# A four-layer mixer kernel: S5's direct term in its convolution kernels, z in three matmuls per block of rows, last state matrices loaded early, S5's parameter steps one head later

## The chip, the cores and the metric

One core of a Trainium2 chip runs the whole program in one launch. The metric is the device time of that launch in microseconds (us), as a median over runs. Engines: PE is TensorE (PEld its weight loads), DVE VectorE, ACT ScalarE, POOL GpSimd, SP SyncE (here only a DMA queue).

## The reference, cut to what matters

Input x is 1 x 256 x 2048, fp32. Four layers follow each other (SSD, FOX, MLA, S5), each a mixer between a residual and a LayerNorm. The change touches SSD's scores, the heads of FOX and above all S5:

```python
def s5_mixer(h, w_in, lam_re, lam_im, log_step, b_re, b_im, c_re, c_im, d_skip, w_glu, b_glu, w_out):
    u, z = jnp.split(h @ w_in, 2, axis=-1)
    ...                                   # lam_bar, b_bar from the parameters, u in groups of 16
    bu = jnp.einsum('gpi,btgi->btgp', b_bar, ug)
    _, states = lax.associative_scan(_diag_linear_combine, (a_seq, bu), axis=1)
    y = jnp.einsum('gip,btgp->btgi', c, states).real.reshape(bsz, T, S5_WIDTH) + d_skip.astype(f32) * u
    y = jax.nn.gelu(y)
    y = y * jax.nn.sigmoid(y @ w_glu.astype(f32) + b_glu.astype(f32))
    y = y * jax.nn.silu(z.astype(f32))
    return y.astype(h.dtype) @ w_out
```

## The kernel before, in words

**Products.** Every fp32 product with a weight is made of three products of halves: high x high, high x low, low x high. A half tile of weights (512 KB, `raw`, 7 buffers) is loaded by SP's queue; ACT rounds it to `whi` (L119) and DVE subtracts to get `wlo` (L120), 4 buffers each. Activations lie transposed, 16 blocks of 128 rows x 256 tokens, as a high and a low part, side by side as well.

`proj_T` (L153) makes 128 output features x 256 tokens: for each of the 16 blocks one 512-wide matmul of `whi` against [high | low] (L147) and one 256-wide matmul of `wlo` against high (L148). The result has two halves of 256 columns, which a DVE reduction adds (L157). `proj_Tk` (L200) has another form, three 256-wide matmuls per block into one sum (L212 to L214), with nothing left to add. `proj_tok` (L160) makes token-major outputs by `mm3` (L126 to L128).

**Order.** The engines' instruction streams are in the order that a scheduler gives them. The kernel's own clock is `C.tick()`: it passes once for each half tile of weights in the projections named here. `C.defer(n, fn)` runs `fn` n ticks later and puts its instructions behind the last matmul issued so far, so that small work of a layer is dealt out among the matmuls.

**SSD.** In each of eight groups `scores` (L557) multiplies the decay matrices `arena` (made at L538) by C·B (L567, DVE); it is deferred by three ticks (L569).

**FOX.** While FOX runs, the parameters of S5 are prepared by a generator, `s5_params`, in 16 turns. One step of it is POOL work for turn n (L1101 to L1126, ending in the matrices `pn`, whose state part is written to `P_d` in DRAM, L1132) and PE work for turn n - 1 (`turn`, L1053: four transposes L1057 and 16 small matmuls L1064 that give the convolution kernels `kt`, copied from PSUM by DVE at L1066). Eight steps are deferred, three come behind v strips, and each head takes one more (L715). POOL also makes the head's mask `ckm` (L714), behind `C.pool_last`, the last step's DMA.

**S5.** Four u strips come first (`proj_Tk`), then 16 tiles of z (`z_tile`, by `proj_T`), each followed by a tanh on ACT and one DVE operation (L1324). Under the matmuls of z run: the state recurrence on DVE (`scan`, L1194 to L1200, four kinds of operations), dealt out by `advance` at SCAN_US = 1.9 of its own estimate per tick; and `outputs`, which takes k = 0 to 7 (four feature tiles ft, two halves each) as soon as the states of the tile are done: `y_near` (kernels against u, L1383), `y_far` (state matrices against states, L1399, added by DVE at L1403), `back1` and `back2` (transposes L1412, L1422). In `back2` DVE adds the direct term D·u (L1428), and one tick later `gelu` follows. Kernels and state matrices for k come by POOL's DMA queue into three buffers of one tag, "mats" (`shifts` L1175, `mats` L1166). After z, PE goes on with the gate's projection (glu), whose tiles take the feature tile ft = 3 last, then with the output layer.

Of the kernel before, what the change touches and what calls it, by code (L numbers as in the profile page):

```python
# [30 lines left out]
class Core:  # L31
# [104 lines left out]
    def proj_T_steps(self, src, hT, ps, m=P, order=range(KB)):  # L136

        mm = self.nc.tensor.matmul
        for i in range(2):
            w = self.half(src, i, KB * m)
            for j in range(8):
                kb = 8 * i + j
                hi, lo = (x[:, j * m:(j + 1) * m] for x in w)
                mm(ps, hi, hT[2][order[kb]], start=kb == 0, stop=False)  # L147
# [303 lines left out]
def ssd(C, hT, out):  # L451
# [3 lines left out]
    with C.tc.tile_pool(name="ssd", bufs=1) as sp, C.tc.tile_pool(name="ssd_c", bufs=1) as vp, C.tc.tile_pool(name="ssd_t", bufs=1) as tp:  # L455
# [87 lines left out]
        def group(g):  # L543
# [25 lines left out]
            C.defer(3, scores)  # L569
# [85 lines left out]
def fox(C, hT, out):  # L655
# [3 lines left out]
    with pool(name="fox", bufs=1) as fp, pool(name="fox_t", bufs=2) as tp, \  # L659
# [49 lines left out]
        def head(h):  # L709
# [5 lines left out]
            C.behind(lambda: next(steps, None))  # L715
# [218 lines left out]
def s5_params(C, sp, sq):  # L934
# [118 lines left out]
    def turn(n, st, pn, d):  # L1053
# [12 lines left out]
        V.tensor_copy(kt[n % 2][:, :, 48:], kp[0:64, 0:128].rearrange("p (e f) -> p e f", e=2))  # L1066
# [74 lines left out]
def s5(C, hT, out):  # L1141
# [8 lines left out]
    with C.tc.tile_pool(name="s5", bufs=1) as sp, C.tc.tile_pool(name="s5_w", bufs=1) as wp, C.tc.tile_pool(name="s5_t", bufs=1) as tp:  # L1150
        dT = sp.tile([P, KB], F32, name="dT")
        bg = sp.tile([P, KB], F32, name="bg")
        nc.sync.dma_start(dT, A["s5_dT"])
# [175 lines left out]
        held = []  # L1329

        def y_load(k):
            ft, h2 = divmod(k, 2)
# [4 lines left out]

        def outputs():
# [92 lines left out]
        def gelu(ft, yf):  # L1431
            y4 = sp.tile([P, 2, 4, T], F32R, tag=f"xu{ft}", name=f"y4{ft}")
            for gq in range(4):
                kb = 4 * gq + ft
                yh[kb], yl[kb], yb[kb] = y4[:, 0, gq], y4[:, 1, gq], y4[:, :, gq]
                g = tp.tile([P, T], F32, tag="gl", name="gl", bufs=2)
                nc.scalar.activation(g.rearrange("p (m k r) -> p r k m", k=4, r=L), yf[gq].rearrange("p (r k m) -> p r k m", r=L, k=4),
                                     AF.Gelu_apprx_tanh)
                C.split(yh[kb], yl[kb], g)
# [53 lines left out]
def prep(inp):  # L1493
# [75 lines left out]
```

## Time and profile before

| | us |
|---|---|
| three runs | 2040.04, 2040.04, 2044.45 (median 2040.04) |
| profiled execution, its own time | 2042.04 |
| its span in the trace | 2040.2 |
| PE busy | 1988.5 (97% of the span) |
| DVE busy | 1472.4 (72%) |
| ACT busy | 957.6 (47%) |
| POOL busy | 409.7 (20%) |

How to read it: the profiled execution lasted 2 us more than the median, so a change of the profiled time is taken over to the median as a difference. Busy times overlap; on PE the ends of matmuls are modelled, so spacings from start to start are safer than durations. The granted clock (PEclk) is 1.00 at 2.4 GHz and 0.50 at 1.2 GHz.

### The profile page before, as it was taken

What the parts mean: (1) busy time and instruction counts of PE and PEld (TensorE: products, weight loads), DVE (VectorE), ACT (ScalarE), POOL (GpSimd) and SP (SyncE); (2) the same over time, 40 slices, a digit from 0 to 9 for tenths busy, and PEclk for the clock granted to TensorE, in tenths of its full rate; (3) what the DMA queues carried; (4) which work ended last, traced back from release to release, by engine and by line L of the source; (5) the groups of instructions that cost most, each with busy time, mean ns of one, the idle gap of its engine ahead of it and who ended that gap; (6) DMA issues with size and microseconds to landing.
All of it is one profiled execution on the core that took longest, in us unless ns stands there. A gap on an engine that the chain in (4) does not pass through costs nothing.

```text
span 2040.2 us, 31823 instructions
## 1 busy us (share of the span) xinstructions
PE 1988.5 (97%) x12073; PEld 1695.5 (83%) x12073; DVE 1472.4 (72%) x2572; ACT 957.6 (47%) x1427; POOL 409.7 (20%) x482
## 2 busy tenths in 40 slices
PE   8999999999999999999999999999999999999997
PEld 6788888888888878788888879888888799778885
DVE  6798887887644695677776567766556678996856
ACT  5455555555433334344444444545554355445542
POOL 0101111001100018999991000000000000110002
PEclk9999999999999999999999999999999999999999
DMA  8555555555665547565666555654347556685652
GB/s 285 186 184 181 185 176 184 186 185 185 218 200 191 181 139 242 182 205 198 197 209 197 180 183 150 205 190 145 104 145 252 174 184 197 171 250 194 196 191 91
DMA packets 116233, 382.40 MB, mean 187 GB/s; under 512 B 18208, under 2 KB 20976, under 8 KB 114288
## 3 DMA queue, kind: packets, MB, share of 16 engines
q1 hardware_dynamic: 103424, 348.11, 52.5%
q0 software_dynamic: 7808, 26.56, 4.2%
q10 hardware_dynamic: 4848, 5.70, 0.8%
q8 instruction: 95, 1.56, 0.3%
q14 instruction: 58, 0.48, 0.1%
HBM read 366.20 MB, written 14.11 MB: 186 GB/s over the span
## 4 chain that ended last, share of the span: by engine, by line
PE 82%; DVE 10%; DMA 3%; POOL 2%; issue 2%; ACT 1%; SPq 0%; DVEq 0%; POOLq 0%; ACTq 0%
PE pT L147 24%; PE pT L148 12%; PE pt L127 10%; PE pt L126 10%; PE pt L128 10%; DVE wlo L120 3%; PE pk L212 2%; PE pk L214 2%; PE pk L213 2%; PE yd L602 1%; PE lps L898 1%; PE lps L897 1%; DVE hres L339 1%; DVE hres L340 1%; PE o L444 1%
## 5 line engine op out<-in xcount | busy, mean ns | idle before, releaser
L120 DVE TENSOR_TENSOR wlo<-raw,whi 128x1024 fp32r<-128x1024 f32 (+4 forms) x612 | 751.5, 1230 | 340.4 <-ACT whi L119 336.4
L119 ACT CAST whi<-raw 128x1024 fp32r<-128x1024 f32 (+4 forms) x612 | 632.0, 1036 | 730.9 <-PE pt L128 316.9
L147 PE MATMUL pT<-h,whi 128*128 128x512 f32 (+2 forms) x2080 | 744.8, 401 | 0.0
L148 PE MATMUL pT<-h,wlo 128*128 128x256 f32 (+2 forms) x2080 | 585.4, 281 | 3.0 <-DVE wlo L120 3.0
L147 PEld LDWEIGHTS pT<-h,whi 128*128 128x128 f32 (+2 forms) x2080 | 389.6, 187 | 92.8 <-issue 0.2
L148 PEld LDWEIGHTS pT<-h,wlo 128*128 128x128 f32 (+2 forms) x2080 | 392.2, 189 | 4.8 <-DVE wlo L120 3.8
L126 PE MATMUL pt<-whi,h 128*128 128x512 f32 (+2 forms) x716 | 281.0, 393 | 6.5 <-ACT whi L119 6.1
L127 PE MATMUL pt<-wlo,h 128*128 128x512 f32 (+2 forms) x716 | 279.3, 390 | 5.4 <-DVE wlo L120 5.3
L128 PE MATMUL pt<-whi,h 128*128 128x512 f32 (+2 forms) x716 | 276.6, 386 | 0.3 <-DVE h L357 0.3
L127 PEld LDWEIGHTS pt<-wlo,h 128*128 128x128 f32 x716 | 135.9, 190 | 35.2 <-DVE wlo L120 8.4
L126 PEld LDWEIGHTS pt<-whi,h 128*128 128x128 f32 x716 | 135.5, 190 | 34.5 <-ACT whi L119 6.5
L128 PEld LDWEIGHTS pt<-whi,h 128*128 128x128 f32 x716 | 135.8, 190 | 26.9 <-issue 1.7
L589 POOL TENSOR_TENSOR xs<-xs,dsk 128x512 f32<-128x512 f32 x16 | 20.8, 1318 | 372.6 <-ACT xs L585 372.6
L126 PE MATMUL pt<-whi,yh 128*128 128x512 f32 x240 | 95.5, 398 | 0.0
L127 PE MATMUL pt<-wlo,yh 128*128 128x512 f32 x240 | 95.4, 397 | 0.0
L128 PE MATMUL pt<-whi,yl 128*128 128x512 f32 x240 | 94.9, 395 | 0.0
L147 PE MATMUL pT<-y,whi 128*128 128x512 f32 x256 | 90.0, 395 | 0.0
L1166 POOL DMA_DIRECT2D mats<-W_d x8 | 4.3, 539 | 355.6 <-DVE h L292 285.3
L148 PE MATMUL pT<-y,wlo 128*128 128x256 f32 x256 | 72.2, 282 | 0.0
L496 DVE SCALAR_TENSOR_TENSOR conv<-u,cw,conv 128x255 f32<-128x255 f32 x144 | 69.0, 480 | 2.2
L89 POOL MEMSET mask<- 128x256 f32 x2 | 0.6, 314 | 301.3 <-PE pt L128 164.4
L147 PEld LDWEIGHTS pT<-y,whi 128*128 128x128 f32 x256 | 48.3, 189 | 10.7 <-DVE y L292 0.3
(469 smaller groups left out, 3093.4 us busy)
## 6 DMA issues: line engine op xcount, KB each, us to landing
raw<-in_ssd_x SPq DMA_DIRECT2D x64, 512.0 KB
raw<-in_ssd_o SPq DMA_DIRECT2D x64, 512.0 KB
raw<-in_ssd_z SPq DMA_DIRECT2D x63, 512.0 KB
raw<-in_fox_v SPq DMA_DIRECT2D x32, 512.0 KB
raw<-in_fox_q SPq DMA_DIRECT2D x32, 512.0 KB
raw<-in_fox_k SPq DMA_DIRECT2D x32, 512.0 KB
raw<-in_fox_z SPq DMA_DIRECT2D x32, 512.0 KB
raw<-in_fox_o SPq DMA_DIRECT2D x32, 512.0 KB
```

The lines of the kernel that those rows point to most:

```text
L119: nc.scalar.copy(hi[:, c], r[:, c])
L120: nc.vector.tensor_tensor(lo[:, c], r[:, c], hi[:, c], op=ALU.subtract)
L126: mm(ps, s[0], m[0], start=first, stop=False)
L127: mm(ps, s[0], m[1], start=False, stop=False)
L128: self.last = mm(ps, s[1], m[0], start=False, stop=last).ins
L147: mm(ps, hi, hT[2][order[kb]], start=kb == 0, stop=False)
L148: self.last = mm(ps[:, 0], lo, hT[0][order[kb]], start=False, stop=kb == KB - 1).ins
L212: mm(o, ws[0], a[0], start=kb == 0 and c % 2 == 0, stop=False)
L213: mm(o, ws[0], a[1], start=False, stop=False)
L214: self.last = mm(o, ws[1], a[0], start=False, stop=end).ins
L496: nc.vector.scalar_tensor_tensor(c[:, k:], u[:, 0:T - k], cw[:, ti, 3 - k:4 - k], c[:, k:], op0=ALU.mult, op1=ALU.add)
L589: nc.gpsimd.tensor_tensor(heads(xs[c]), heads(xs[c]), bc(dsk, g), op=ALU.mult)
```

## The change

1. SSD: `scores` of the first group is deferred by 6 ticks, those of the others by 3 as before.
2. FOX: head 0 takes no step of S5's parameters, so each later step falls one head later.
3. S5's direct term: D is added to the first 16 x 16 block of each convolution kernel. Each turn copies 48 of the 64 columns and adds `eye`·`skip` to the other 16 by two small DVE operations. `back2` loses its DVE operation, and gelu reads PSUM there at once, a tick earlier.
4. z by `proj_T3`: three 256-wide matmuls per block into one sum, no reduction; tanh and the DVE operation read PSUM.
5. The state matrices of ft = 3 go by POOL's queue into a buffer of their own (the place of `XA`), both halves when k = 6 is loaded; k = 7 waits five ticks and `finish` one.
6. SCAN_US is 2.2, so more of the recurrence is dealt out per tick.

The numbers of lines grow by 9 behind L152, and by more further on.

```diff
+    def proj_T3(self, src, hT, ps):
+        for i in range(2):
+            w = self.half(src, i)
+            for j in range(8):
+                kb = 8 * i + j
+                self.mm3(ps, [x[:, j * P:(j + 1) * P] for x in w], [x[kb] for x in hT[0:2]], kb == 0, kb == KB - 1)
+            self.tick()
...
-            C.defer(3, scores)
+            C.defer(3 if g else 6, scores)
...
-            C.behind(lambda: next(steps, None))
+            if h:
+                C.behind(lambda: next(steps, None))
...
+    eye, skip = sq.tile([64, 16], F32, name="eye"), sq.tile([64, 32], F32, name="skip")
+    nc.sync.dma_start(skip, A["s5_dk"])
+    V.tensor_tensor(eye, C.ident[0:64, 0:16], C.ident[0:64, 16:32], op=Ad)
+    for k0 in (32, 48):
+        V.tensor_tensor(eye, eye, C.ident[0:64, k0:k0 + 16], op=Ad)
...
-        V.tensor_copy(kt[n % 2][:, :, 48:], kp[0:64, 0:128].rearrange("p (e f) -> p e f", e=2))
+        V.tensor_copy(kt[n % 2][:, :, 64:], kp[0:64, 0:128].rearrange("p (e f) -> p e f", e=2)[:, :, 16:])
+        for e in range(2):
+            V.scalar_tensor_tensor(kt[n % 2][:, e, 48:64], eye, skip[:, 2 * n + e:2 * n + e + 1], kp[0:64, e * 64:e * 64 + 16], op0=M, op1=Ad)
...
-            C.proj_T(A["s5_z"][kb], hT, zs[kb])
+            zps = C.acc("zps")[:, 0:T]
+            C.proj_T3(A["s5_z"][kb], hT, zps)
...
-            nc.scalar.activation(th, zs[kb], AF.Tanh, scale=0.5)
-            nc.vector.scalar_tensor_tensor(zs[kb], th, 1.0, zs[kb], op0=ALU.add, op1=ALU.mult)
+            nc.scalar.activation(th, zps, AF.Tanh, scale=0.5)
+            nc.vector.scalar_tensor_tensor(zs[kb], th, 1.0, zps, op0=ALU.add, op1=ALU.mult)
...
-            pm = mats(C.P_d[ft].rearrange("p h c j f -> p h (c j f)")[:, 2 * h2:2 * h2 + 2]).rearrange(
...
+            if ft < 3:
+                pm = mats(src)
+            else:
+                if h2 == 0:
+                    rest.append(sp.tile([P, 2, 1024], F32, tag="XA", name="mats3"))
+                pm = rest[0][:, h2]
+                nc.gpsimd.dma_start(pm, src)
...
-            wait = 4 if k == 6 else 3 if k < 6 else 1
+            wait = 4 if k == 6 else 5 if k == 7 else 3
...
-                    if held:
-                        held[0] = (7, C.now) + held[0][2:]
-                    else:
-                        C.defer(3, finish)
+                    if not held:
+                        C.defer(1, finish)
...
-                    nc.vector.scalar_tensor_tensor(dst, uX[ft][:, :, gq], dT[:, kb:kb + 1], src[:, a], op0=ALU.mult, op1=ALU.add)
-            C.defer(1, lambda: gelu(ft, yf))
...
+                    nc.scalar.activation(g.rearrange("p (m k r) -> p r k m", k=4, r=L), src[:, a], AF.Gelu_apprx_tanh)
+                    C.split(yh[kb], yl[kb], g)
...
-SCAN_US = 1.9
+SCAN_US = 2.2
```

Where the scheduler now puts the instructions is shown at three places. **First, DVE at the end of SSD's first group** (`conv` and `xc` are the causal convolution, `arena` the decay matrices). Before:

```order
L496 SCALAR_TENSOR_TENSOR conv<-u,cw,conv 128x255
L538 SCALAR_TENSOR_TENSOR arena<-arena,tok,upm 128x128 x16
L567 TENSOR_TENSOR arena<-arena,cbp 128x1024 x2
L496 SCALAR_TENSOR_TENSOR conv<-u,cw,conv 128x254
L157 TENSOR_REDUCE u<-pT 128x256
L496 SCALAR_TENSOR_TENSOR conv<-u,cw,conv 128x253
L120 TENSOR_TENSOR wlo<-raw,whi 128x1024
L499 SCALAR_TENSOR_TENSOR xc<-xc,conv 128x256
```

Now:

```order
L505 SCALAR_TENSOR_TENSOR conv<-u,cw,conv 128x255
L547 SCALAR_TENSOR_TENSOR arena<-arena,tok,upm 128x128 x16
L505 SCALAR_TENSOR_TENSOR conv<-u,cw,conv 128x254
L576 TENSOR_TENSOR arena<-arena,cbp 128x1024
L505 SCALAR_TENSOR_TENSOR conv<-u,cw,conv 128x253
L576 TENSOR_TENSOR arena<-arena,cbp 128x1024
L508 SCALAR_TENSOR_TENSOR xc<-xc,conv 128x256
L166 TENSOR_REDUCE u<-pT 128x256
L120 TENSOR_TENSOR wlo<-raw,whi 128x1024
```

Both products of `scores` still stand ahead of the next `wlo`, and the `xc` operation that stood behind it stands ahead of it too.

**Second, PE at the start of FOX's head 0** (`wp`, `kp` are the transposes and kernels of a turn; `pT` begins the head's q). Before:

```order
L126 MATMUL pt_7235<-whi,h_6497 128x512
L127 MATMUL pt_7235<-wlo,h_6497 128x512
L128 MATMUL pt_7235<-whi,h_6497 128x512
L1057 MATMUL wp<-ident,wn 128x2x64 x4
L1064 MATMUL kp<-pn,bd_6979 32x64 x8
L1057 MATMUL wp<-ident,wn 128x2x64 x4
L1064 MATMUL kp<-pn,bd_6978 32x64 x8
L147 MATMUL pT<-h_6344,whi 128x512
L148 MATMUL pT<-h_6344,wlo 128x256
```

Now:

```order
L126 MATMUL pt_7243<-whi,h_6497 128x512
L127 MATMUL pt_7243<-wlo,h_6497 128x512
L128 MATMUL pt_7243<-whi,h_6497 128x512
L1073 MATMUL wp<-ident,wn 128x2x64 x4
L1080 MATMUL kp<-pn,bd_6979 32x64 x8
L147 MATMUL pT<-h_6344,whi 128x512
L148 MATMUL pT<-h_6344,wlo 128x256
```

One turn is left there; the second stands at the start of head 1, and so on.

**Third, POOL's issues for S5** (`shifts` are the kernels, `mats` the state matrices, `hres` belongs to the last LayerNorm). The last rows before:

```order
L1175 DMA shifts<-K_d 64x1x848 x2
L1166 DMA mats<-P_d 128x1024
L1175 DMA shifts<-K_d 64x1x848 x2
L1166 DMA mats<-P_d 128x1024
L328 TENSOR_TENSOR hres<-hres,gb_19673 128x512
```

Now:

```order
L1191 DMA shifts<-K_d 64x1x848 x2
L1358 DMA mats_18166<-P_d 128x1024 x2
L1182 DMA mats<-P_d 128x1024
L1191 DMA shifts<-K_d 64x1x848 x2
L1182 DMA mats<-P_d 128x1024
L1191 DMA shifts<-K_d 64x1x848 x2
L1182 DMA mats<-P_d 128x1024
L1191 DMA shifts<-K_d 64x1x848 x4
L337 TENSOR_TENSOR hres<-hres,gb_19932 128x512
```

The two loads of ft = 3's state matrices (`mats_18166`) stand ahead of three other pairs of loads; the last thing in the queue is now a load of kernels.

## Rows read from the trace of the kernel before

**Rows 1.** The page, busy time of each engine, share of the span and number of instructions.

```profile
PE 1988.5 (97%) x12073; PEld 1695.5 (83%) x12073; DVE 1472.4 (72%) x2572; ACT 957.6 (47%) x1427; POOL 409.7 (20%) x482
```

**Rows 2.** PE's waits over the whole span: waiting line, what it waited for, us in total, times, longest.

```profile
PE pt L127 <- DVE wlo L120: 5.8, 6, 3.0
...
PE far L1399 <- DMA mats<-P_d: 3.7, 1, 3.7
PE far L1399 <- DVE yt L1428: 3.0, 1, 3.0
PE pT L148 <- DVE wlo L120: 3.0, 2, 1.5
PE kp L1064 <- POOL pn L1119: 2.8, 1, 2.8
PE yp L1412 <- DVE ys L1403: 2.8, 1, 2.8
PE kp L1064 <- POOL pn L1126: 2.2, 1, 2.2
```

**Rows 3.** Windows: stretch, its length, busy us and instructions of PE, PEld, DVE, ACT and POOL, then PE's granted clock, the DMA share and GB/s.

```profile
819.30:825.80 6.50, 5.33 (x27) 4.58 (x28) 0.28 (x1) 0.00 (x0) 6.09 (x13) 0.50 0.51 151
1809.20:1812.30 3.10, 3.10 (x14) 2.60 (x11) 2.86 (x13) 2.51 (x6) 1.23 (x2) 0.50 0.30 80
1843.20:1849.90 6.70, 5.62 (x79) 5.16 (x80) 0.75 (x2) 1.06 (x2) 0.00 (x0) 0.50 0.30 88
1713.30:1808.00 94.70, 86.05 (x982) 74.62 (x980) 92.41 (x206) 43.46 (x70) 9.64 (x16) 1.00 0.67 194
```

**Rows 4.** PE's timeline inside a z tile: start, duration, line, operation. The first two rows are two pairs apart, the last two three pairs.

```profile
1810.13 0.63 PE L147 MATMUL pT<-h,whi 128*128 128x512 f32 x1
...
1811.41 0.63 PE L147 MATMUL pT<-h,whi 128*128 128x512 f32 x1
...
1812.92 0.40 PE L147 MATMUL pT<-h,whi 128*128 128x512 f32 x1
...
1813.98 0.40 PE L147 MATMUL pT<-h,whi 128*128 128x512 f32 x1
```

**Rows 5.** POOL's timeline near the end of z; in brackets the idle time before and what ended it.

```profile
1821.83 1.23 POOL L1175 DMA_DIRECT2D shifts<-K_d  x2 [0.42 <-PE far L1399]
1835.89 0.58 POOL L1166 DMA_DIRECT2D mats<-P_d  x1 [12.82 <-PE near L1383]
```

**Rows 6.** PE's timeline at the end of z.

```profile
1844.28 1.99 PE L1399 MATMUL far<-X,mats 64*64 64x64 f32 x64 [3.68 <-DMA mats<-P_d]
...
1849.88 1.07 PE L1422 MATMUL yp<-ident,yt 128*128 128x128 f32 x8
```

**Rows 7.** DVE's groups from 1713.3 to 1808.1 us: line, operation, shapes, count, busy us and mean ns, idle before.

```profile
L157 DVE TENSOR_REDUCE zs<-pT 128x256 f32<-128x512 f32 x12 | 8.2, 685 | 0.0
...
L1428 DVE SCALAR_TENSOR_TENSOR yt<-xu,dT,yp 128x256 f32<-128x256 f32 x7 | 3.0, 474 | 0.0
```

**Rows 8.** DVE's timeline in the same stretch; from start to start is what an operation takes from DVE.

```profile
1748.48 0.68 DVE L157 TENSOR_REDUCE zs<-pT 128x256 f32<-128x512 f32 x1
1749.08 0.68 DVE L1196 TENSOR_TENSOR sc<-X,a4s 128x512 f32<-128x512 f32 x1
1749.68 0.42 DVE L1324 SCALAR_TENSOR_TENSOR zs<-th,zs 128x256 f32<-128x256 f32 x1
1750.02 0.69 DVE L1198 TENSOR_TENSOR sc<-sc 128x512 f32<-128x512 f32 x1
1750.62 1.22 DVE L120 TENSOR_TENSOR wlo<-raw,whi 128x1024 fp32r<-128x1024 f32 x1
1751.75 0.69 DVE L1200 TENSOR_TENSOR X<-X,sc 128x512 f32<-128x512 f32 x1
```

**Rows 9.** PE's timeline in a u strip of S5, first and last of 22 matmuls that follow each other without a gap.

```profile
1646.12 0.28 PE L214 MATMUL pk<-h,wlo 128*128 128x256 f32 x1
...
1648.64 0.28 PE L214 MATMUL pk<-h,wlo 128*128 128x256 f32 x1
```

**Rows 10.** Weight loads of the same u strips: count, duration in ns (least, median, most), first and last start.

```profile
L212 PEld LDWEIGHTS pk<-h,whi x192: 186/192/192, 1630.3 to 1712.8; 128*128 128x128 f32 x192
```

**Rows 11.** A DVE operation of MLA of the kind that z has now, one input in PSUM.

```profile
L907 DVE SCALAR_TENSOR_TENSOR yf<-o,zs x16: 424/425/425, 1419.6 to 1524.5; 128x256 f32<-128x256 f32 x16
```

**Rows 12.** PE's timeline from the start of FOX's head 0 to head 2.

```profile
814.54 0.66 PE L1057 MATMUL wp<-ident,wn 128*128 128x128 f32 x4
817.99 0.30 PE L1064 MATMUL kp<-pn,bd 128*32 128x64 f32 x2 [2.79 <-POOL pn L1119]
820.47 1.28 PE L1064 MATMUL kp<-pn,bd 128*32 128x64 f32 x14 [2.19 <-POOL pn L1126]
...
841.84 0.89 PE L1064 MATMUL kp<-pn,bd 128*32 128x64 f32 x16
...
861.90 0.89 PE L1064 MATMUL kp<-pn,bd 128*32 128x64 f32 x16
```

**Rows 13.** POOL's timeline over the same heads, the last operation of three steps.

```profile
819.57 0.86 POOL L1126 TENSOR_TENSOR pn<-t,t 128x320 f32<-128x320 f32 x1
...
836.42 1.75 POOL L1126 TENSOR_TENSOR pn<-t,t 128x320 f32<-128x320 f32 x1
...
856.14 0.88 POOL L1126 TENSOR_TENSOR pn<-t,t 128x320 f32<-128x320 f32 x1
```

**Rows 14.** The DVE copy of each turn.

```profile
L1066 DVE COPY kt<-kp x16: 272/274/285, 791.0 to 1083.8; 64x128 f32<-64x128 f32 x16
```

**Rows 15.** DVE's timeline at the end of SSD's first group.

```profile
72.38 2.34 DVE L567 TENSOR_TENSOR arena<-arena,cbp 128x1024 f32<-128x1024 f32 x2
...
76.03 1.22 DVE L120 TENSOR_TENSOR wlo<-raw,whi 128x1024 fp32r<-128x1024 f32 x1
77.16 0.42 DVE L499 SCALAR_TENSOR_TENSOR xc<-xc,conv 128x256 f32<-128x256 f32 x1
77.50 0.48 DVE L496 SCALAR_TENSOR_TENSOR conv<-u,cw,conv 128x255 f32<-128x255 f32 x1
```

**Rows 16.** PE's timeline at the same place.

```profile
77.30 0.51 PE L127 MATMUL pt<-wlo,h 128*128 128x512 f32 x1 [2.98 <-DVE wlo L120]
```

More of the change, by code (lines that the diff above doesn't have):

```diff
@@ L1150, in s5 @@
     with C.tc.tile_pool(name="s5", bufs=1) as sp, C.tc.tile_pool(name="s5_w", bufs=1) as wp, C.tc.tile_pool(name="s5_t", bufs=1) as tp:
-        dT = sp.tile([P, KB], F32, name="dT")
         bg = sp.tile([P, KB], F32, name="bg")
-        nc.sync.dma_start(dT, A["s5_dT"])
         nc.sync.dma_start(bg, A["s5_bgT"])
@@ L1333, in y_load @@
             tm = shifts(ft, h2)
-            pm = mats(C.P_d[ft].rearrange("p h c j f -> p h (c j f)")[:, 2 * h2:2 * h2 + 2]).rearrange(
-                "p (g c q e f) -> p g c q e f", g=2, c=2, q=2, e=2)
-            held.append((k, C.now, tm, pm))
+            src = C.P_d[ft].rearrange("p h c j f -> p h (c j f)")[:, 2 * h2:2 * h2 + 2]
+            if ft < 3:
[5 more added lines that the diff above has]
+                nc.gpsimd.dma_start(pm, src)
+            held.append((k, C.now, tm, pm.rearrange("p (g c q e f) -> p g c q e f", g=2, c=2, q=2, e=2)))
         def outputs():
             k, since, tm, pm = held[0]
-            wait = 4 if k == 6 else 3 if k < 6 else 1
+            wait = 4 if k == 6 else 5 if k == 7 else 3
             if C.now >= since + wait and (k > 5 or PIECE[k // 2] in done):
@@ L1356, in outputs @@
                     rest.append(pm)
-                    if held:
-                        held[0] = (7, C.now) + held[0][2:]
-                    else:
-                        C.defer(3, finish)
+                    if not held:
+                        C.defer(1, finish)
             if held:
                 C.defer(1, outputs)
-        rest = []
         def finish():
@@ L1369, in finish @@
             for h2 in range(2):
-                y_far(3, h2, rest[h2])
+                y_far(3, h2, rest[1 + h2])
         def y_near(ft, h2, tm):
@@ L1417, in back2 @@
         def back2(ft, yt):
-            yf = [yt[:, gq // 2].rearrange("p r g i -> p (r g i)")[:, gq % 2 * T:(gq % 2 + 1) * T] for gq in range(4)]
+            y4 = sp.tile([P, 2, 4, T], F32R, tag=f"xu{ft}", name=f"y4{ft}")
             for hq in range(2):
@@ L1422, in back2 @@
                     tr(yp3[:, r * P:(r + 1) * P], yt[:, hq, r].rearrange("p g i -> p (g i)"), C.ident)
-                src = yp3.rearrange("p (r a c) -> p a r c", r=L, a=2)
+                src = yp3.rearrange("p (r a k m) -> p a r k m", r=L, a=2, k=4)
                 for a in range(2):
@@ L1426, in back2 @@
                     kb = 4 * gq + ft
-                    dst = yf[gq].rearrange("p (r c) -> p r c", r=L)
-                    nc.vector.scalar_tensor_tensor(dst, uX[ft][:, :, gq], dT[:, kb:kb + 1], src[:, a], op0=ALU.mult, op1=ALU.add)
-            C.defer(1, lambda: gelu(ft, yf))
[L1431 to L1439, printed above, removed]
+                    yh[kb], yl[kb], yb[kb] = y4[:, 0, gq], y4[:, 1, gq], y4[:, :, gq]
+                    g = tp.tile([P, T], F32, tag="gl", name="gl", bufs=2)
+                    nc.scalar.activation(g.rearrange("p (m k r) -> p r k m", k=4, r=L), src[:, a], AF.Gelu_apprx_tanh)
+                    C.split(yh[kb], yl[kb], g)
             ready.append(ft)
@@ L1540, in prep @@
     o["s5_o"] = k_blocks(g["s5_w_out"][0])
-    o["s5_dT"] = np.ascontiguousarray(g["s5_d"][0].reshape(KB, P).T)
+    o["s5_dk"] = np.ascontiguousarray(g["s5_d"][0].reshape(2, 2, 16, 2, 16).transpose(0, 1, 4, 2, 3).reshape(64, 32))
     o["s5_bgT"] = np.ascontiguousarray(g["s5_b_glu"][0].reshape(KB, P).T)
```

2 lines of the change are left out of this document (1 added, 1 removed).

## The prediction

> **What bounds the kernel now.** The page's busy times come first: PE is busy for 1988.5 us of the span of 2040.2, DVE for 72% of it [rows 1]. So only two things can shorten the program: less work on PE, or fewer of the moments in which PE waits or runs at half its clock. PE's list of waits gives the moments [rows 2]. In FOX it waits 2.8 + 2.2 us for POOL's `pn`. Under S5's z it waits twice for `wlo` (3.0), once for `ys` (2.8) and once for `yt` (3.0), all DVE's, and at the end of z 3.7 us for a DMA of state matrices. In SSD there is one wait of 3.0 us for `wlo`. The windows then show what follows such a wait: in 819.3 to 825.8, 1809.2 to 1812.3 and 1843.2 to 1849.9 the granted clock is 0.50, the 1.2 GHz level [rows 3]. What that costs is read from one z tile: two pairs of matmuls take 1.28 us at half clock (0.64 a pair), three pairs 1.06 us at full clock (0.353 a pair) [rows 4]. Each microsecond of PE work spent at half clock thus loses 1 - 0.353/0.64 = 0.45 us.
>
> **FOX (part 2).** PE issues two turns in a row at the start of head 0. The second stands at 814.5 and needs matrices that POOL only ends at 819.57 + 0.86 = 820.4 [rows 12, 13]. Now it stands at the start of head 1. Head 1's own turn was at 841.8 before [rows 12]; without 5 us of waits, 2.4 of slow clock and one turn of some 1.5 us that is about 833, 12 us after `pn` is there. The next one comes a head later (a head takes 861.90 - 841.84 = 20.1 us), at about 853, and its `pn` ended at 836.42 + 1.75 = 838.2 before. POOL's steps then follow each other in 18 to 20 us [rows 13], no slower than the heads, so the lead stays. The mask of head 1 now goes ahead of a step on POOL, which only makes it earlier. Behind the turn PE has the head's q and k, which no longer wait. Removed: 2.8 + 2.2 = 5.0 us of waits. The half clock from 820.5 to 825.8 goes with them: 5.3 x 0.45 = 2.4. **Part 2: -7.4.** Its bounds are 0, if the wait returns a head later, and -7.4.
>
> **z and the recurrence (parts 3, 4, 6).** From 1713.3 to 1808.0 DVE is busy for 92.4 of 94.7 us and PE for 86.05 [rows 3], so DVE sets the pace, and PE's four waits add up to 3.0 + 2.8 + 3.0 = 8.8. What an operation takes from DVE is its spacing, 0.08 less than its duration: the reduction 0.60, the z operation 0.34, `wlo` 1.13 [rows 8].
> - The 12 reductions of the stretch go: 12 x 0.60 = 7.2. The 7 `yt` operations go [rows 7]: 7 x 0.39 = 2.8.
> - The recurrence is the same work, but with 2.2 for 1.9 per tick it ends after 24 x 1.9/2.2 = 21 half tiles of z where it took 24. Three half tiles slip behind the crowded stretch: 3 x 1.13 of `wlo` and 1.5 x 0.34, together 3.9.
> - DVE then needs 94.7 - 7.2 - 2.8 - 3.9 = 80.8. PE needs 86.05 less 24 pairs of 0.353, that is 77.6, and 168 blocks in the new form add 1.2: 78.8. DVE still has 2.0 more to do, and I leave that as waits. Of 8.8, 6.8 go.
> - The half clock from 1809.2 to 1812.3 follows the wait for `yt`; it goes: 3.1 x 0.45 = 1.4.
> - PE's own work grows. A block takes three 256-wide matmuls for one of 512 and one of 256. The u strips of S5 have that form: 21 spacings in 2.52 us, 0.120 each, 0.360 a block against 0.353 [rows 9, 4]. 16 tiles x 16 blocks x 0.007 = +1.8.
> - The z operation reads PSUM now. MLA has the same operation with an input in PSUM: 0.424 us [rows 11], against 0.42 in z [rows 8]. Nothing. Tanh on ACT stands beside it and has no one waiting.
>
> The weight loads need a look, because the new form has three per block for two. In the u strips a load of 128 columns takes 192 ns [rows 10], longer than the 120 ns from one matmul to the next: loads run under matmuls, and the third one is not paid separately. The Trainium skill ("TensorE: Matmul & The Clock Gate", section "The mechanism") says that a weight load overlaps matmuls in flight only when it targets other rows of the array, and its section "LDWEIGHTS (loading the stationary operand)" gives a load as columns / 1.2 ns, 107 ns here; by that rule 256 more loads of full height would cost an estimated 27 us, and part 4 would lose. The trace disagrees, with 192 ns loads at 120 ns spacing, so the measured spacing stands in my sum.
>
> **The end of z (part 5).** The last `mats` load is issued at 1835.89, when a near product frees a buffer [rows 5], and `far` starts at 1844.28 after 3.7 us of waiting [rows 6]: some 8.4 us from issue to use. In the new order both halves are requested ahead of three other pairs of loads, two tiles earlier, so `far` finds them. Last in the queue is now the kernel load for k = 7. The like of it was issued at 1821.8 before [rows 5], and k = 7 comes five half tiles later, 5 x 8 x 0.36 = 14.4 us; 8.4 us to land leave 6. The wait of 3.7 goes, and the half clock from 1844.3 to 1849.9: 5.6 x 0.45 = 2.5. The transposes of the last tile, which stood behind z with nothing else to run, now stand among its last halves. The moved loads fall where the DMA share is 0.67 [rows 3] and no wait of PE is for a raw tile; I cost them at nothing. **Parts 3 to 6: -6.8 - 1.4 + 1.8 - 3.7 - 2.5 = -12.6.**
>
> **SSD (part 1) and small things.** The order shows both products of `scores` (2.34 us together) still ahead of the `wlo` for which PE waits 2.98 us [rows 15, 16], and the `xc` operation, 77.50 - 77.16 = 0.34 [rows 15], now ahead of it too. So the wait stays and grows: +0.3, with -3.0 as the other bound, if three ticks more let the products finish early after all. The first `eye` operation falls into SSD's LayerNorm, where DVE works alone: +0.3, bounded by 0 and by the 0.27 us of a larger copy [rows 14]. Each turn's copy of 0.27 becomes a smaller copy and two small operations, at most 2 x 0.42 by the kind in [rows 11]: up to 16 x 0.85 = 13.6 us of DVE. They run within FOX heads, where only the store to DRAM waits for `kt`; PE's waits for DVE there do not appear [rows 2]. Nothing; without that cover, up to 13.6.
>
> **The sum** is made against the profiled execution's 2042.04: -7.4 - 12.6 + 0.3 + 0.3 = -19.4, giving 2022.6. The median of the runs, 2040.04, lies 2.0 below the profiled one; -19.4 from it gives **2020.6**.
>
> **Rivals.**
> - *DVE still sets the pace in z.* The new rate of the recurrence puts 0.3 more on each half tile, as much as half a reduction takes off. If PE's waits come from the queue in front of `wlo`, `ys` and `yt`'s successors rather than from the sum, 8.2 us (6.8 + 1.4) do not come back: 2020.6 + 8.2 = 2028.8. For it: 80.8 against 78.8 is close. Against it: the small matmuls of the y products give PE the same work over fewer half tiles. Chance 0.13.
> - *FOX gives nothing back*, because POOL's step falls behind a head again: 2028.0. Against it the 12 us of lead. Chance 0.06.
> - *The end of z waits for another load*, the kernels of k = 7, now last in the queue: 6.2 us stay, 2026.8. Against it the margin of 6 us. Chance 0.07.
> - *The first two together*: 2020.6 + 8.2 + 7.4 = 2036.2, not to be told from no change. Chance 0.07.
> - *Slower: the third weight load of a block is not hidden in z.* Place: every block of z, 256 of them; price 0.19 us each [rows 10], +48.6, hence 2069.2. It decides against the change once more than 19.4/256 = 0.076 us of each extra load lies bare. Against it are the u strips, of the same form [rows 9]. Chance 0.03.
> - That the change does not do what it says holds for part 1 by the order, and is in the sum.
>
> **How the numbers follow.** My forecast has 0.62, the rivals 0.36, and 0.02 is left for a loss that I cannot name. The range runs from 2015 (no wait left in z, -2.0; SSD's wait gone, -3.3; no `eye` cost, -0.3) to 2031 (the first three rivals, each with the 2 us by which the profiled execution and the median differ). Outside are the two together, the slower ones and some 0.04 of the forecast's own tails. A measurement can tell 0.3% from no change, 6.1 us, so faster means under 2033.9: 0.62 + 0.13 + 0.06 + 0.07 = 0.88; same 0.07; slower 0.05.
>
> **What would show it.** Right: PE's waits without `pn`, with no `mats` DMA at the last `far`; granted clock 1.00 in FOX's head 0 and at the end of z; z blocks of three matmuls at 0.36 us; PE's waits under z about 2 us, DVE without reductions there; SSD's 3.0 us wait still there, some 0.3 longer. Wrong: waits of 5 us or more for DVE under z (first rival); a turn in head 1 or 2 that waits for `pn` (second); a near product of k = 7 that waits for its DMA (third); z blocks at 0.4 us or more (slower).

## The result and the profile after

| | before | changed | ratio, 95% interval |
|---|---|---|---|
| first measurement, median us | 2040.04 | 2026.24 (2022.86 to 2029.47) | 0.9924 (0.9910 to 0.9937) |
| second, another chip | 2041.42 | 2023.12 (2020.58 to 2025.52) | 0.9908 (0.9893 to 0.9922) |
| profiled execution, own time | 2042.04 | 2022.86 | |

The kernel is faster by 13.8 us in the first measurement and by 18.3 in the second; 19.4 were forecast. Times of the changed kernel scatter by 5 to 7 us, those of the kernel before by up to 12, so single profiles are compared stage by stage here, with the start times of the same matmul in both traces:

| stage, us | before | after | difference | forecast |
|---|---|---|---|---|
| start to the end of SSD's first group | 102.9 | 99.7 | -3.2 | +0.3 |
| from there to FOX's head 0 | 709.9 | 710.0 | +0.1 | +0.3 |
| start of head 0 | 18.0 | 9.0 | -9.0 | -7.4 |
| the other heads (with the turn moved there, +1.3) | 278.3 | 276.9 | -1.4 | in the row above |
| attention's output, MLA, S5's strips | 604.3 | 604.3 | 0.0 | 0 |
| z and the first eight blocks of glu | 139.2 | 131.9 | -7.3 | -12.6 |
| the rest | 174.1 | 175.8 | +1.7 | 0 |

So the sum of the profiled execution came out as forecast (-19.1 of the trace, -19.4 forecast) with two of its terms wrong: z gave 5 us less, and SSD and FOX's heads gave some 6 that I had not seen. That the sum fits so well is luck in part: the profiled execution was the fastest of its four, and the medians give 13.8 and 18.3. The page's busy times, against [rows 1]:

```profile
PE 1982.8 (98%) x12329; PEld 1704.3 (84%) x12329; DVE 1465.1 (72%) x2575; ACT 955.1 (47%) x1427; POOL 406.7 (20%) x482
```

PE has 256 matmuls more and is busy 6 us less: less of its work runs at half clock, and FOX's matmuls follow each other faster. PE's waits over the whole span, against [rows 2]:

```profile
PE yp L1431 <- DVE ys L1422: 3.0, 2, 2.4
PE xp L585 <- DVE xc L508: 2.6, 2, 1.7
PE pt L127 <- DVE wlo L120: 2.3, 4, 0.8
PE yp L1431 <- DVE sc L1214: 2.0, 1, 2.0
```

The waits for `pn`, for `yt` and for the DMA of `mats` are gone. Under z the wait of the y transposes for `ys` stands there with 5.0 us in all (the 2.0 put down to `sc` is the same wait: the addition to `ys` stands in DVE's queue behind the recurrence). The windows, against [rows 3] (length, busy us of PE, PEld, DVE, ACT, POOL, granted clock, DMA share, GB/s):

```profile
808.00:830.00 22.00, 22.00 (x142) 18.89 (x141) 13.00 (x15) 9.90 (x13) 21.00 (x28) 1.00 0.66 213
1699.90:1801.40 101.50, 97.01 (x1368) 94.79 (x1367) 98.20 (x228) 47.68 (x80) 13.21 (x22) 0.98 0.67 195
1774.80:1784.80 10.00, 8.01 (x82) 7.63 (x80) 9.21 (x42) 4.41 (x8) 0.00 (x0) 0.83 0.59 180
1825.00:1832.00 7.00, 7.00 (x54) 6.58 (x52) 3.53 (x5) 5.28 (x12) 0.00 (x0) 1.00 0.81 216
```

Head 0 and the end of z run at full clock without a gap. In z DVE is still full until the recurrence ends (98.2 of 101.5 us), and behind the second wait the clock falls again: 0.83 over 10 us is 3.4 us at half clock, 1.5 us of PE's time.

FOX's turns on PE and the matrices that the second needs on POOL, against [rows 12, 13]:

```profile
810.67 0.89 PE L1080 MATMUL kp<-pn,bd 128*32 128x64 f32 x16
829.75 0.89 PE L1080 MATMUL kp<-pn,bd 128*32 128x64 f32 x16
```

```profile
817.54 0.88 POOL L1144 TENSOR_TENSOR pn<-t,t 128x320 f32<-128x320 f32 x1
```

The second turn stands in head 1, 11 us after its `pn` (12 were forecast). A z tile on PE, against [rows 9], the first and last of 27 matmuls in a row:

```profile
1752.79 0.28 PE L126 MATMUL zps<-h,whi 128*128 128x256 f32 x1
...
1755.91 0.28 PE L128 MATMUL zps<-h,wlo 128*128 128x256 f32 x1
```

26 spacings in 3.12 us are 0.120 each, 0.360 a block, as forecast. The weight loads of the same tiles take 192 ns, against [rows 10]:

```profile
L126 PEld LDWEIGHTS zps<-h,whi x256: 186/192/330, 1699.8 to 1827.6; 128*128 128x128 f32 x128
```

The end of z, against [rows 6]:

```profile
1815.16 1.15 PE L1402 MATMUL near<-xu,shifts 64*64 64x64 f32 x32
1819.31 2.10 PE L1418 MATMUL far<-X,mats 64*64 64x64 f32 x128
```

No wait stands before either: the matrices and the last kernels are there. SSD's first group, against [rows 16]:

```profile
74.15 0.44 PE L585 MATMUL xp<-ident,xc 128*128 128x128 f32 x2 [1.73 <-DVE xc L508]
```

A wait of 1.7 us for `xc` has taken the place of 3.0 for `wlo`. Both go back to one DMA: DVE can't begin the decay matrices, which stand ahead of `scores`' products, `xc` and `wlo`, before their input has landed. First before, then after:

```profile
68.17 4.29 DVE L538 SCALAR_TENSOR_TENSOR arena<-arena,tok,upm 128x128 f32<-128x128 f32 x16 [3.04 <-DMA arena<-acs_d]
```

```profile
66.42 4.29 DVE L547 SCALAR_TENSOR_TENSOR arena<-arena,tok,upm 128x128 f32<-128x128 f32 x16 [2.74 <-DMA arena<-acs_d]
```

The DMA landed 1.8 us earlier here. And how the wait for `ys` comes about, first PE, then DVE:

```profile
1736.22 1.10 PE L1418 MATMUL far<-X,mats 64*64 64x64 f32 x62
...
1745.86 0.84 PE L1431 MATMUL yp<-ident,ys 128*128 128x128 f32 x6 [2.36 <-DVE ys L1422]
```

```profile
1742.89 1.22 DVE L120 TENSOR_TENSOR wlo<-raw,whi 128x1024 fp32r<-128x1024 f32 x1
1744.03 0.69 DVE L1216 TENSOR_TENSOR X<-X,sc 128x512 f32<-128x512 f32 x1
1744.63 0.41 DVE L1341 SCALAR_TENSOR_TENSOR zs<-th,zps 128x256 f32<-128x256 f32 x1
1744.96 0.75 DVE L1422 TENSOR_TENSOR ys<-ys,far 128x256 f32<-128x256 f32 x2
```

The far products end at 1737.3; DVE comes to their addition 7.6 us later, having done weights and recurrence without a pause, and PE waits 2.4 us for it.

### The profile page after: what moved, and what is told of

The parts are those of the page before. It is cut to its first block, busy times and chain, and to the rows that moved or that the text cites. A ratio compares the mean times of both kernels' runs of the same rounds, so it can differ in the third digit from the quotient of the medians.

```text
span 2021.1 us, 32370 instructions
## 1 busy us (share of the span) xinstructions
PE 1982.8 (98%) x12329; PEld 1704.3 (84%) x12329; DVE 1465.1 (72%) x2575; ACT 955.1 (47%) x1427; POOL 406.7 (20%) x482
## 4 chain that ended last, share of the span: by engine, by line
PE 84%; DVE 11%; DMA 2%; issue 2%; ACT 1%; SPq 0%; DVEq 0%; ACTq 0%; POOLq 0%
PE pT L147 22%; PE pT L148 11%; PE pt L127 11%; PE pt L126 11%; PE pt L128 11%; DVE wlo L120 3%; PE pk L221 2%; PE pk L222 2%; PE pk L223 2%; PE yd L611 1%; PE lps L908 1%; PE lps L907 1%; DVE hres L348 1%; DVE hres L349 1%; PE o L453 1%
## 5 line engine op out<-in xcount | busy, mean ns | idle before, releaser
L147 PE MATMUL pT<-h,whi 128*128 128x512 f32 (+1 forms) x1824 | 647.4, 398 | 0.0
L148 PE MATMUL pT<-h,wlo 128*128 128x256 f32 (+1 forms) x1824 | 510.7, 280 | 0.0
L147 PEld LDWEIGHTS pT<-h,whi 128*128 128x128 f32 (+1 forms) x1824 | 339.8, 186 | 79.9
L148 PEld LDWEIGHTS pT<-h,wlo 128*128 128x128 f32 (+1 forms) x1824 | 341.7, 187 | 1.0
L126 PEld LDWEIGHTS pt<-whi,h 128*128 128x128 f32 x716 | 135.3, 189 | 34.4 <-ACT whi L119 6.4
L126 PE MATMUL zps<-h,whi 128*128 128x256 f32 x256 | 74.9, 293 | 0.0
L127 PE MATMUL zps<-h,whi 128*128 128x256 f32 x256 | 73.1, 285 | 0.0
L128 PE MATMUL zps<-h,wlo 128*128 128x256 f32 x256 | 73.0, 285 | 0.0
```

Source lines behind the costliest of these rows:

```text
L126: mm(ps, s[0], m[0], start=first, stop=False)
L127: mm(ps, s[0], m[1], start=False, stop=False)
L128: self.last = mm(ps, s[1], m[0], start=False, stop=last).ins
```

## The experiments

Each edit is against the changed kernel unless the text says otherwise. The runs stood on three chips, each against the kernel before on the same chip; only scan19, fox_now and pad64 stood on the chip of the second measurement. The changed kernel itself gave ratios of 0.9924 and 0.9908, so a ratio near these says nothing about a part, and the profiles must.

"z" below is z with the first eight blocks of glu in the profile: 139.2 us before, 131.9 changed. It scatters too. Five profiles have the changed kernel's z (the first, again, pad64, fox_now, scores3): three took 131.8 to 131.9 us, and two 133.4, as the clock fell behind the last wait there. In fox_now (length, busy us of PE, PEld, DVE, ACT, POOL, granted clock, DMA share, GB/s):

```profile
1815.00:1825.00 10.00, 9.02 (x66) 8.92 (x68) 5.41 (x9) 5.01 (x11) 0.00 (x0) 0.83 1.00 378
```

Ahead of that wait the clock makes no difference. The addition on DVE that ends it starts 102.8 to 102.9 us into z in all five, whose clock fell ahead of it once, at one of two places, and in late_pd, whose clock did not fall in z at all. In again (z's first matmul at 1697.81) and in late_pd (at 1704.23):

```profile
1800.64 0.75 DVE L1422 TENSOR_TENSOR ys<-ys,far 128x256 f32<-128x256 f32 x2
```

```profile
1807.10 0.74 DVE L1424 TENSOR_TENSOR ys<-ys,far 128x256 f32<-128x256 f32 x2
```

So DVE sets the pace for these 103 us: what half clock costs PE there is taken off its next wait. Behind them a fall costs z 1.5 us.

**The changed kernel again (again).**

> The changed kernel once more. Median between 2022.9 and 2029.5 us, ratio to the kernel before 0.991 to 0.994. In the profile PE waits some 5 us for ys under z. Two theories on the pace of matmuls: if the place of operands in memory sets it, a pair takes 353 ns in the glu stage and 350 in FOX's heads, as in the first profile; if it is set anew in each run, these values change.

2023.12 us, ratio 0.9908 (0.9893 to 0.9922); z 131.8, waits for `ys` 5.0. Glu's pairs again 353 ns, FOX's heads 349. This is the measure for the runs below.

**The recurrence dealt out as before (scan19).**

```diff
-SCAN_US = 2.2
+SCAN_US = 1.9
```

> The changed kernel with SCAN_US 1.9. Theory A: the recurrence at 2.2 per tick puts DVE behind PE in z, so at 1.9 the waits for ys (5.0 us) fall under 1.5, the half clock after them goes, and the kernel is 3 to 5 us faster than the changed one. Theory B: the wait comes from the place of the y transposes, two ticks behind the far products, whatever DVE's load: waits stay at 4 us or more, time within 1.5 us of the changed one. A third possibility: the recurrence ends too late for the last far products, which then wait at the end of z: 3 us or more slower.

2027.04 us, 0.9923 (0.9908 to 0.9937), no gain. PE's waits:

```profile
PE yp L1431 <- DVE sc L1212: 3.2, 1, 3.2
...
PE yp L1431 <- DVE ys L1422: 2.8, 2, 2.5
```

6.0 us for 5.0; z is 133.3, with 2.6 us lost at half clock behind the longest wait, so part 6 is worth 1.5 us at most, and theory A falls. No wait of the last far products appears, so the third possibility falls too. DVE is as full, and the recurrence ends 103.7 us into z for 101.5: the rate sets when the kernel lets the products of a finished tile follow, hardly when DVE does the recurrence, which the order puts wherever DVE is free.

**The steps back at head 0 (fox_now).**

```diff
-            if h:
-                C.behind(lambda: next(steps, None))
+            C.behind(lambda: next(steps, None))
```

> The changed kernel with the parameter steps back at head 0. If part 2 is worth what its waits show: 7.4 us slower than the changed one, with waits of 2.8 and 2.2 us for pn and a granted clock of 0.50 for some 5 us behind them. Rival: FOX pays for it elsewhere, and the difference is under 4 us.

2033.22 us, 0.9957 (0.9943 to 0.9971), 10.1 slower than the changed kernel on the same chip.

```profile
PE kp L1079 <- POOL pn L1136: 2.8, 1, 2.8
PE kp L1079 <- POOL pn L1143: 2.1, 1, 2.1
```

Both waits are back, and so is the half clock:

```profile
814.00:820.00 6.00, 3.07 (x20) 2.47 (x21) 0.62 (x4) 0.10 (x1) 5.81 (x9) 0.50 0.53 154
```

The start of head 0 takes 17.0 us for 9.0, the other heads 275.7 for 276.9 (one turn fewer there): part 2 is worth 6.8 us in FOX, of 7.4 forecast. The two profiles differ by 16.7 us, as this one was the slowest of its six; the rest lies mostly in MLA and S5's strips (some 6 us) and in z (1.6), where nothing was changed. So the 10.1 is not all part 2.

**A 64-byte tile where D was (pad64).**

```diff
+        dT = sp.tile([P, KB], F32, name="dT")
+        nc.vector.memset(dT, 0.0)
         bg = sp.tile([P, KB], F32, name="bg")
```

> The changed kernel with a 64-byte tile in the place of the removed D, so that S5's tiles lie where they lay before; it is set to zero once and not used. If the place of the activations sets the pace of glu's matmuls: a pair takes 346.7 ns again instead of 353.3, 1.7 us faster. If not: glu's pairs are as in the changed kernel, and the time is the same.

2023.43 us, 0.9909 (0.9896 to 0.9923); the same time within the scatter, but glu's matmuls are faster. The changed kernel's glu, ten pairs apart:

```profile
1861.79 0.40 PE L147 MATMUL pT<-y,whi 128*128 128x512 f32 x1
...
1865.32 0.40 PE L147 MATMUL pT<-y,whi 128*128 128x512 f32 x1
```

and with the tile:

```profile
1861.80 0.40 PE L147 MATMUL pT<-y,whi 128*128 128x512 f32 x1
...
1865.27 0.40 PE L147 MATMUL pT<-y,whi 128*128 128x512 f32 x1
```

0.353 and 0.347 a pair; the rest of glu takes 85.9 us for 87.5.

**The y transposes two ticks later (back4).**

```diff
-                C.defer(2 if ft < 3 else 1, lambda: back1(ft, ys[ft]))
+                C.defer(4 if ft < 2 else 2 if ft < 3 else 1, lambda: back1(ft, ys[ft]))
```

> The changed kernel with the first y transposes of ft = 0 and 1 four ticks behind the far products instead of two. Theory B, their place: the waits for ys (5.0 us) go, nothing takes their place, and z with its half clock is 5 to 6.6 us shorter. Theory C, DVE's load: DVE has more to do than PE until the recurrence ends, so PE waits for wlo or another of its results instead; the time is within 2 us of the changed kernel's on the same chip.

2027.45 us, 0.9928 (0.9914 to 0.9941).

```profile
PE near L1402 <- DVE ys L1422: 4.8, 1, 4.8
...
PE far L1418 <- issue: 1.5, 1, 1.5
```

The transposes no longer wait; the near products of k = 5 do, for DVE's addition of the far products of k = 4, which comes 16 us behind them. z is 134.6. Theory B falls.

**z's tanh and DVE operation under glu (zlater).**

```diff
-            th = tp.tile([P, T], F32, tag="th", name="th", bufs=3)
-            nc.scalar.activation(th, zps, AF.Tanh, scale=0.5)
-            nc.vector.scalar_tensor_tensor(zs[kb], th, 1.0, zps, op0=ALU.add, op1=ALU.mult)
+            nc.scalar.copy(zs[kb], zps)
```

(tanh and the operation stand at the head of each glu tile then)

> The changed kernel with z's tanh and its DVE operation moved under glu; ACT copies z from PSUM. Nine of these operations, 9 x 0.33 = 3.0 us, leave the stretch in which DVE is full. Theory C (load): the waits under z fall by some 3 us and the half clock after the second one goes, 3 to 4.6 us faster than the changed kernel. Theory B (place): the waits stay at 4 us or more, time within 1.5 us.

2027.64 us, 0.9925 (0.9912 to 0.9938).

```profile
PE yp L1429 <- DVE ys L1420: 3.1, 1, 3.1
...
PE yp L1429 <- DVE sc L1214: 2.1, 1, 2.1
```

With 3 us less for DVE the waits are 5.2 and z is 132.9. Theory C, as I had put it, falls too. Where the freed time goes is seen in the window from z's first matmul to the end of the recurrence, first the changed kernel (again), then this one:

```profile
1697.80:1799.20 101.40, 96.93 (x1367) 94.72 (x1366) 98.10 (x228) 47.75 (x80) 13.21 (x22) 0.98 0.68 196
```

```profile
1700.80:1797.30 96.50, 91.28 (x1233) 89.35 (x1232) 92.84 (x215) 44.90 (x76) 12.01 (x20) 0.96 0.66 197
```

DVE is 96 to 97% busy in both. The recurrence ends 4.9 us earlier, and PE waits as long.

**z by pairs with the reduction (z_pairs).**

```diff
-            zps = C.acc("zps")[:, 0:T]
-            C.proj_T3(A["s5_z"][kb], hT, zps)
+            zps = zs[kb]
+            C.proj_T(A["s5_z"][kb], hT, zps)
```

> Part 4 undone: z by pairs of matmuls and DVE's reduction again. By the load of DVE: 16 reductions of 0.60 come back, some 11 of them where DVE is full, +6.6, less 1.8 that PE saves: 4 to 6 us slower than the changed kernel. Rival: the reductions were hidden, then PE's saving alone counts, 1 to 2 us faster.

2021.69 us, 0.9906 (0.9891 to 0.9920): as fast as the changed kernel. PE's waits:

```profile
PE yp L1431 <- DVE ys L1422: 4.5, 2, 3.3
...
PE far L1418 <- issue: 1.5, 1, 1.5
```

Sixteen reductions more leave the waits at 6.0 for 5.0 and z at 130.6, 1.2 less than with three matmuls; the clock fell once in both, where that costs nothing. The recurrence ends 108.6 us into z for 101.5. The rival was right: the reductions were hidden but for 1.0 us of waits, and part 4 costs what PE pays.

**The state matrices late again (late_pd).** The edit takes back part 5 of the diff, with its waits.

```diff
-            if ft < 3:
+            if True:
...
-            wait = 4 if k == 6 else 5 if k == 7 else 3
+            wait = 4 if k == 6 else 3 if k < 6 else 1
...
-                        C.defer(1, finish)
+                        C.defer(3, finish)
```

> Part 5 undone: the last state matrices share the three buffers again, k = 7 waits one tick from k = 6 and finish three. If part 5 is worth what the row showed: a wait of 3 to 4 us for the mats DMA at the last far products and half clock behind it, 5 to 6.5 us slower than the changed kernel. Rival: with the recurrence dealt out faster the loads come earlier too and are there in time, under 2 us slower.

2028.66 us, 0.9929 (0.9912 to 0.9946).

```profile
PE yp L1433 <- DVE ys L1424: 5.7, 3, 2.4
...
PE yp L1433 <- DVE sc L1214: 2.0, 1, 2.0
```

The DMA's wait does not return. The third wait for `ys` is new: 1.25 us for the last addition, behind z. The waits are 7.7 us for 5.0, and the clock did not fall in this z at all:

```profile
1704.20:1837.70 133.50, 125.64 (x1763) 121.82 (x1762) 114.90 (x253) 64.17 (x110) 13.30 (x22) 1.00 0.71 217
```

z is 133.4. Its first 103 us are those of the changed kernel, as shown above; behind them it takes 1.5 us more, most of it the new wait. That is what part 5 is worth beside the others, since the rest already brings the end of the recurrence, and with it the loads, forward. The rival was right; the timed difference from the changed kernel, 4 us by the ratios, lies between two chips, and the intervals overlap.

**The far additions by ACT and POOL (ypool).**

```diff
             for b in range(2):
-                nc.vector.tensor_tensor(y[:, b::2], y[:, b::2], far[b][:, 0:4 * NC].rearrange("p (g c) -> p g c", g=4), op=ALU.add)
+                fs = tp.tile([P, T], F32, tag="gl", name="fs", bufs=2).rearrange("p (g c) -> p g c", g=4)
+                nc.scalar.copy(fs, far[b][:, 0:4 * NC].rearrange("p (g c) -> p g c", g=4))
+                nc.gpsimd.tensor_tensor(y[:, b::2], y[:, b::2], fs, op=ALU.add)
```

> The changed kernel with the 16 additions of the far products taken off DVE: ACT copies them from PSUM, POOL adds them. Theory D: PE's waits for ys come from DVE's queue, where the additions stand behind whatever of the recurrence is ready, so they neither fall with DVE's load (zlater) nor with the transposes' place (back4). Then they go here: z with the start of glu falls from 131.8 to 126 us or less, the kernel is 5 to 6.5 us faster than the changed one. Theory C, DVE's load as such: PE waits for wlo instead, z stays over 129 us, time within 2 us.

2030.71 us, 0.9952 (0.9934 to 0.9969): slower than the second measurement of the changed kernel.

```profile
PE zps L128 <- DVE wlo L120: 5.3, 6, 1.5
```

No wait for DVE's `ys` is left, and z is 136.3 all the same: PE waits six times for `wlo`, and 1.9 us more for ACT. Theory D falls as I had put it: here it is `wlo`, the next thing PE asks of DVE, that is late. That is theory C's sign, though its 2 us for the time are exceeded.

**The same with pairs and the tile (ypool_pairs_pad).** The edits of ypool, z_pairs and pad64 together.

> The same, with z by pairs of matmuls and the reduction (part 4 undone) and the 64-byte tile of pad64. By theory D the reductions are hidden once no result that PE waits for stands in DVE's queue: 1 to 3 us faster than the kernel with POOL's additions alone, and 1.7 more in glu from the place of the tiles; z with the start of glu under 125 us. If DVE's load counts: z over 129 us.

2030.11 us, 0.9947 (0.9929 to 0.9964). z is 139.9, so theory D's 125 fails here too; PE waits 9.4 us for POOL's `ys`, once 5.8, where DVE's own addition kept it waiting 2.4 at most. Glu is at 85.9 us again, as in pad64.

**Two small tiles in the kernel before (before_pad).** Against the kernel before:

```diff
     kt = [sq.tile([64, 2, 112], F32, name=f"kt{n}") for n in range(2)]
+    eye, skip = sq.tile([64, 16], F32, name="eye"), sq.tile([64, 32], F32, name="skip")
+    V.memset(eye, 0.0)
+    V.memset(skip, 0.0)
```

> The kernel before with the two small tiles of the change (64 x 16 and 64 x 32) allocated in FOX, set to zero and not used, so that POOL's and DVE's tiles behind them move by 192 bytes. All kernels of the change run FOX's heads with pairs of 348.7 to 349.1 ns, the kernel before with 353.4. If the place of the tiles does it: 349 here, and FOX's heads 2.4 to 2.8 us shorter. If not: 353 and the time of the kernel before.

2038.96 us against 2040.94, 0.9988 (0.9978 to 0.9998). FOX's heads take 275.7 us for 278.3. The same place in both, first before:

```profile
866.01 0.40 PE L147 MATMUL pT<-h,whi 128*128 128x512 f32 x1
...
868.13 0.40 PE L147 MATMUL pT<-h,whi 128*128 128x512 f32 x1
```

and with the tiles:

```profile
867.28 0.40 PE L147 MATMUL pT<-h,whi 128*128 128x512 f32 x1
...
869.36 0.40 PE L147 MATMUL pT<-h,whi 128*128 128x512 f32 x1
```

Six pairs take 2.12 us there and 2.08 here; the mean over the heads is 353.4 and 348.9 ns. But glu, whose own tiles the edit does not move, ran at 353.3 in this profile and at 346.7 before, so the place is not all.

**SSD's scores three ticks behind (scores3).**

```diff
-            C.defer(3 if g else 6, scores)
+            C.defer(3, scores)
```

> Part 1 undone: scores of SSD's first group three ticks behind. As forecast, part 1 costs 0.3 us: the changed kernel's time within 1 us, with one wait of 3 us for wlo near 77 us. Rival, from the profiles after: the change took away that wait and the half clock behind it for a shorter wait for xc, and it is worth 1 to 2.5 us: that much slower here, with a granted clock of 0.50 near 80 us.

2027.36 us, 0.9935 (0.9918 to 0.9952).

```profile
PE pt L127 <- DVE wlo L120: 6.0, 5, 2.9
```

The wait of 2.9 us is back, and the stretch to the end of the first group is 100.7 us. But that stretch scatters more than this: in the eleven profiles with part 1 it takes 98.3 to 102.5 us, and in the two others without it 102.9 and 102.4. What sets it is when the DMA lands for which DVE waits. DVE begins the decay matrices at 65.1 to 67.9 us in the eleven, and PE's wait for `xc` grows with that from 0 to 2.8 us. From this start to the end of the stretch 33.1 to 33.2 us pass in all profiles whose clock does not fall there, with part 1 or without, and 34.4 to 34.7 in the five where it falls. ypool, which has part 1, and scores3 even began at the same time. DVE and PE in ypool, then DVE in scores3:

```profile
67.61 4.29 DVE L547 SCALAR_TENSOR_TENSOR arena<-arena,tok,upm 128x128 f32<-128x128 f32 x16 [3.76 <-DMA arena<-acs_d]
75.34 0.33 PE L585 MATMUL xp<-ident,xc 128*128 128x128 f32 x1 [2.76 <-DVE xc L508]
```

```profile
67.61 4.29 DVE L547 SCALAR_TENSOR_TENSOR arena<-arena,tok,upm 128x128 f32<-128x128 f32 x16 [3.00 <-DMA arena<-acs_d]
```

The waits are 2.8 and 2.9 us, and both reach the end of the group within 0.1 us of each other. So these runs show no gain of part 1 and no loss; the forecast and its rival are both off. The timed difference lies on another chip, with an interval that holds the changed kernel's first ratio, 0.9924.

## Why the prediction was right, and where it was wrong

**FOX (part 2) was right in mechanism and size.** The waits for `pn` and the half clock went, the turn stands 11 us behind its matrices, and fox_now brings the waits and the half clock back: 6.8 us measured for 7.4.

**The pace of FOX's heads was not in the sum.** Pairs there are 348.7 to 349.1 ns in every kernel after and 353.4 before, 2.6 us in all. It does not come from part 2, as fox_now has it too; before_pad gains 2.6 us there by two unused tiles.

**z: the step that failed is "the recurrence is the same work", and with it the figure of 80.8 for DVE and the 2.0 of waits.** (That figure also starts from the length of the stretch, 94.7, and not from DVE's busy time, 92.4.) PE's figure, 78.8, held: from z's first matmul to the fifth far products 84.7 us passed, with 4.4 of waits and 1.5 lost at half clock. But in that stretch DVE did four operations each of the recurrence more (39 for 35), 5.1 us, in the time that the reductions left. The order lets the recurrence fill whatever DVE has free, so DVE stays 96 to 98% busy until the recurrence is through, 118.5 us into z before and 101.5 after. Before:

```profile
1713.30:1831.80 118.50, 109.73 (x1252) 95.53 (x1251) 115.54 (x261) 55.80 (x89) 12.68 (x21) 0.99 0.67 199
```

What DVE does for PE comes late in that time. Relief (zlater), an additional load (z_pairs), another rate (scan19), another place of the transposes (back4) leave 5 to 7 us of waits, and moving the additions off DVE (ypool) turns them into waits for `wlo`. So the first rival was half right: 5.0 us of waits stay where I had left 2.0, and a half clock; 5 us or more was the sign I had given for it. That the last of these waits ends 103 us into z whatever the clock does says the same: there DVE sets the pace, and PE waits for whatever its own work leaves of that time. So the 1.4 that I charged for the half clock after `yt` is not shown to have been there to gain; in before_pad the clock fell once more than before, 47 us into z, and the same addition still started 109.6 us into z for 109.7. Why DVE's own time changes so little from edit to edit is not settled, and no run set the addition further ahead in DVE's order, which would have tried the queue as the cause directly.

**Part 4 brings nothing.** I counted its reductions as relief for PE; they were hidden. PE pays 0.360 a block, as forecast, against pairs at 0.350 on the mean in z before (I had 0.353): 256 x 0.010 = 2.6 us. z_pairs shows 1.2 less in z; the rest of the 2.6 falls where DVE sets the pace. The slower rival fell: in z, as in the strips, loads of 192 ns run under matmuls that follow each other in 120 ns. The rule of the Trainium skill ("TensorE: Matmul & The Clock Gate", section "The mechanism") that a load overlaps matmuls in flight only where it targets other rows is not borne out by z, whose loads all have full height; the same section also lets a load into the background weight buffer go ahead, which would fit, but no run here shows which buffer a load uses.

**Parts 5 and 6** work as said, at 1.5 us and at most 1.5 beside the others, each by one profile. The wait of 3.7 us and its half clock are gone, but late_pd shows no DMA wait without part 5 either: I had charged the whole to a load that the earlier recurrence brings forward anyway. What is left of z's 7.3 us, 5.5 or more, is by difference part 3 and what the parts do together; part 3 was not tried alone.

**SSD (part 1): 3.2 us came where +0.3 was forecast, and they are not shown to be part 1's.** PE's order moved, which I had not read: the transposes of `xc` now stand ahead of the matmuls that need the `wlo`, so PE waits for `xc` instead. But the wait comes from a DMA, which was no term of my sum. It landed 1.8 us earlier in this profile than before, and the half clock of some 1.5 us behind the wait was missing; together that is the 3.2. From DVE's start on the stretch takes the same time with part 1 and without it, as scores3 shows. (The half clock is missing in scores3 too, and three profiles with part 1, back4, zlater and late_pd, have it, so it is not put to this part.) The lower bound of -3.0 took this in by luck.

**The rest:** glu's pairs went from 346.7 to 353.3 ns, 1.4 to 1.7 us, by the 64 bytes that D's tile left (pad64 undoes it).

Errors of opposite sign thus made a sum that fits better than its terms: z gave 5.3 us too little and glu lost 1.7, while FOX's pace (2.6) and SSD (3.5), neither of them a gain that I had costed, made up for it. That is luck.

## What to carry to other kernels

Where a scheduler may move a long chain of deferrable work into an engine's free time, taking work off that engine ends the chain earlier; here it did not make that engine's answers to the others come sooner. Cost such an engine by its queue in front of the waited-for instruction, not by its sum over a stretch. Read the order of the engine that waits as well as of the one that is waited for. Undo each part of a change alone (here one of six parts cost more than it brought), and look first at how much the stretch varies between profiles in which nothing of it was changed: here that was 1.5 us in z and 4 us in SSD, as much as the parts that were to be measured.

## What the runs showed of the hardware

The same stream of matmuls runs at one of a few paces: glu's pairs at 346.7 or 353.3 ns for the whole stage, FOX's heads at about 349 or 353.4 on the mean. In glu it is 353.3 in the kernels whose S5 tiles lie 64 bytes lower, and 346.7 in both kernels with the 64-byte tile and in the kernel before, though before_pad had 353.3 with these tiles unmoved. In MLA, with the tiles unmoved, a stretch takes 207.1 us in most profiles and 208.6 in four (scan19, fox_now, z_pairs, late_pd). So the place of tiles takes part, something else does too, and what it is stays open; it makes 1.4 to 2.6 us a stage, as much as some of the parts above.
